# A step of its own for the decay sums' load, and 56 stores issued from ScalarE's queue

## The chip, the core and the metric

The kernel runs on one core of a Trainium2 chip. The core has a matrix engine (TensorE, PE in the profile), a vector engine (VectorE, DVE), an activation engine (ScalarE, ACT), GpSimd (POOL) and a queue engine that only issues transfers (SyncE, SP). Each engine works through its own list of instructions in order and waits on semaphores for the others. The metric is device time in microseconds (us): lower is better.

## What is computed

One layer over 128 context tokens and 1024 latent tokens. The part that the change touches, cut from the reference:

```
p = h @ w_in   -> [fourier_in | fourier_gate | ssd_z | ssd_xBC | dt | merge_gate_f | merge_gate_s]
f_out = ((fourier_mix(u_f) @ fnet_w) * silu(g_f)) @ w_branch_f
# state-space branch, per chunk c of 128 tokens, group g, head r, both directions:
acs   = cumsum(dt * a)                                # the decay sums
lmat  = exp(where(tri, acs[l] - acs[s], -inf))        # the masked decay
y     = (C_l . B_s) * lmat * xdt  +  C_l . state_in * exp(acs)
s_out = grouped_rmsnorm((y + xs * d_skip) * silu(z)) @ w_branch_s
merged = sigmoid(mg_f) * f_out + sigmoid(mg_s) * s_out
```

The final states of the context (`new_state_ssd_*`) are outputs too; the kernel stores them as `sout`, one tile for each of the 8 groups.

## The kernel before

All products are made of float32 values split in a high and a low part, three matmuls for one (`mm3`, L99). Every column block of `w_in` goes through `gemm` (L206): 24 steps of three matmuls, 128x384, for each third of the 1152 tokens. Between steps it calls `tick()` (L202), which advances a clock and runs whatever was booked for that time with `at(step, ticks)` (L192): the step is a generator, and each tick that it was given runs it to its next `yield`. This fixes the order of TensorE's instructions. The other engines, SP among them, get their order from a scheduler at build time, which works from what the code issued, its data and its buffers.

The state-space part is a loop over 8 groups (L643). In each, `states` (L542) makes the running states and, for k = -1, the context's final state: ScalarE copies it from PSUM to `so` (L557) and a transfer stores it (L558). `outputs` (L568) makes the outputs of one chunk in three steps: (1) load the decay sums `ab` (512 KB, broadcast over the partitions) and the factors `ea`, mask `ab` into `e` on GpSimd (L582, L583), eight exponentials on ScalarE (L586), and add the two directions on VectorE (L587); (2) multiply by `cb`; (3) the matmuls `po` and `y` (L597, L605). The nine chunks of a group come in the order 0, 4, 5, 3, 6, 2, 7, 1, 8, three ticks apart. The tiles `ab` and `so` share two buffers, and `e` has three (shared with `xhl`), `ea` three.

`gate_out` (L160) takes a gate's products from PSUM: ScalarE writes tanh into `gt`; for kind "f" (the Fourier gates, 24 tiles) VectorE then finishes it, for kind "m" (the merge gates, 48 tiles) ScalarE's result is final. Each tile of 192 KB is stored to DRAM (L168). Five merge gates are computed before the groups, one with group 4, two with group 5, one each with groups 6 and 7, and six after the last group, beside the first work of the Fourier stage (L685 on).

All transfers but nine loads from GpSimd's queue are issued from SP's queue. They are given eight completion counters in turn (DMAHW0 to DMAHW7); a transfer that takes a counter waits until the transfer that had it last has landed, unless that is known already.

Of the kernel before, what the change touches and what calls it, by code (L numbers as in the profile page):

```python
# [24 lines left out]
TH = 384  # L25
# [37 lines left out]
def tile_step(ctx, tc, a, o):  # L63
    nc = tc.nc

    ctx.enter_context(tc.manual_schedule(engines={mybir.EngineType.PE}))
    V, S, G, PE = nc.vector, nc.scalar, nc.gpsimd, nc.tensor
# [4 lines left out]
    def act(out, in_, func, bias=0.0, scale=1.0, **kw):  # L72
        S.activation(out, in_, func, bias=bias, scale=scale, **kw)  # L73

    def stt(out, in0, scalar, in1, op0, op1):
        V.scalar_tensor_tensor(out, in0, scalar, in1, op0=op0, op1=op1)

    def tt(out, in0, in1, op):
        V.tensor_tensor(out, in0, in1, op=op)
# [38 lines left out]
    def gt_(name, n=TH + 1):  # L118
        return gq.tile([P, TH + 2], F32, tag="gt", name=name)[:, 0:n]
# [40 lines left out]
    def gate_out(g, it):  # L160

        chunk, kind, dst, i = g
        for t, ps in it:
            gt = gt_(f"gt{chunk}_{t}", TH)
            act(gt, ps, AF.Tanh, scale=0.5)
            if kind == "f":
                stt(gt, gt, 1.0, ps, ALU.add, ALU.mult)
            nc.sync.dma_start(dst[i][:, t * TH : (t + 1) * TH], gt)  # L168

    def gate(n):  # L170
        for _ in range(min(n, len(gates))):
# [20 lines left out]
    def at(step, *ticks):  # L192

        for t in ticks:
            events[clock[0] + t].append(step)
# [40 lines left out]
    with pool("sp") as sp:  # L236
# [84 lines left out]
        for j in range(8):  # L321
            a8, b32 = j // 2 % 2 * 8, j % 2 * 32
            for n0, r0, nr, c0, nc_ in ((0, 1, 3, 0, 32), (96, 0, 1, 1, 15), (111, 4, 1, 1, 15)):
                dst = perm[:, j, n0 : n0 + nr * nc_].rearrange("p (r c) -> p r c", c=nc_)
# [6 lines left out]
                if cols[0] == 0:  # L331
                    G.tensor_copy(dst[:, :, 0:1], rg[:, rs_, 0:1])
                    dst, cols = dst[:, :, 1:], cols[1:]
# [141 lines left out]
    with pool("sd") as sd, pool("ss") as ss, pool("sx", side="right") as sx:  # L475
# [66 lines left out]
        def states(g, k, xb, bn, sts):  # L542

            cf, cb = (0, 0) if k < 0 else (1 + k, 8 - k)
            xw = ss.tile([P, 2, 256], F32, tag="xw", name=f"xw{g}_{k}", bufs=1)
            xhl = ss.tile([P, 2, 2, 256], F32R, tag="e", name=f"xhl{g}_{k}", bufs=3)
            xh, xl = xhl[:, 0], xhl[:, 1]
            for d, c in ((0, cf), (1, cb)):
                tt(xw[:, d].rearrange("p (j h q) -> p j h q", j=2, h=2), xb[:, c].rearrange("p (j h q) -> p j h q", j=2, h=2),
                   wsv[:, c, d, g, :].rearrange("p (h j) -> p j h", h=2).unsqueeze(3).broadcast_to([P, 2, 2, 64]), ALU.mult)  # L550
            split(xh, xl, xw)
            yield
            ps = gps(f"st{g}_{k}")
            if k < 0:
                mm3(ps, (bn[:, 0, 0], bn[:, 1, 0]), [x.rearrange("p d q -> p (d q)") for x in (xh, xl)], True, True)
                so = ss.tile([P, 1024], F32, tag="ab", name=f"so{g}", bufs=2)[:, 0:512]
                S.copy(so, ps)  # L557
                nc.sync.dma_start(o["sout"][g], so)  # L558
                return
            st = sts[0]  # L560
            for d, c in ((0, cf), (1, cb)):
                mm3(ps[:, d * 256 : d * 256 + 256], (bn[:, 0, c], bn[:, 1, c]), (xh[:, d], xl[:, d]), True, True)
            tt(st[:, k + 1].rearrange("p d (h q) -> p d h q", h=4), st[:, k].rearrange("p d (h q) -> p d h q", h=4),
               decv[:, :, g, :, k].unsqueeze(3).broadcast_to([P, 2, 4, 64]), ALU.mult)
            sv = st[:, k + 1].rearrange("p d q -> p (d q)")
            tt(sv, sv, ps, ALU.add)

        def outputs(g, c, bt, ct, xs, xb, st):  # L568

            cc = slice(col(c), col(c) + P)  # L570
            ab = ss.tile([P, 2, 4, P], F32, tag="ab", name=f"ab{g}_{c}", bufs=2)
            nc.sync.dma_start(ab.rearrange("p d h l -> p d (h l)"),
                              d_acs[c].rearrange("(d g q) l -> g d (q l)", d=2, g=NG)[g].partition_broadcast(P))
            if c > 0:

                ea = ss.tile([P, 2, 2, P], F32, tag="ea", name=f"ea{g}_{c}", bufs=3)
                for r0 in range(2):
                    nc.sync.dma_start(ea[r0 * 64 : r0 * 64 + 64].rearrange("p d j l -> p d (j l)"),
                                      d_eac[c].rearrange("(d g h j) l -> g h d (j l)", d=2, g=NG, h=2)[g, r0].partition_broadcast(64))
            e = ss.tile([P, 2, 4, P], F32, tag="e", name=f"e{g}_{c}", bufs=3)  # L580

            G.affine_select(e[:, 0], ab[:, 0], [[0, 4], [1, P]], ALU.is_ge, -1e30, base=0, channel_multiplier=-1)  # L582
            G.affine_select(e[:, 1], ab[:, 1], [[0, 4], [-1, P]], ALU.is_ge, -1e30, base=0, channel_multiplier=1)  # L583
            for d in range(2):
                for h in range(4):
                    act(e[:, d, h], e[:, d, h], AF.Exp, bias=knv[:, c, d, g, h : h + 1])  # L586
            tt(e[:, 0], e[:, 0], e[:, 1], ALU.add)  # L587
            yield
            pcb = gps(f"cb{g}_{c}")
            PE.matmul(pcb[:, 0:P], bt[:, cc], ct[:, cc], start=True, stop=True)  # L590
            tt(e[:, 0], e[:, 0], pcb[:, 0:P].unsqueeze(1).broadcast_to([P, 4, P]), ALU.mult)
            yield
            if c > 0:
                po = gps(f"po{g}_{c}")
                for d, k in ((0, c - 1), (1, 8 - c)):
                    for j in range(2):
                        PE.matmul(po[:, (2 * d + j) * P : (2 * d + j + 1) * P], st[:, k, d, j * P : j * P + P],  # L597
                                  ct[:, cc], start=True, stop=True)
                tt(ea, po.rearrange("p (d j l) -> p d j l", d=2, j=2), ea, ALU.mult)
                G.tensor_tensor(ea[:, 0], ea[:, 0], ea[:, 1], op=ALU.add)  # L600
            py = gps(f"y{g}_{c}")
            for j in range(2):
                for h in (2 * j, 2 * j + 1):
                    r0 = (h % 2) * 64
                    PE.matmul(py[r0 : r0 + 64, j * P : j * P + P], xb[:, c, h * 64 : h * 64 + 64], e[:, 0, h % 2 * 2 + j],  # L605
                              start=True, stop=True, tile_position=(0, r0))
            tt(xs[:, :, cc], xs[:, :, cc], py[:, 0 : 2 * P].rearrange("p (j l) -> p j l", j=2), ALU.add)
            if c > 0:
                tt(xs[:, :, cc], xs[:, :, cc], ea[:, 0], ALU.add)
# [33 lines left out]
        for g in range(NG):  # L643
            bt = ss.tile([P, PADW + 1], F32, tag="bt", name=f"bt{g}")
            ct = ss.tile([P, PADW + 1], F32, tag="ct", name=f"ct{g}")
            xs = sx.tile([P, 2, PADW + 1], F32, tag="xs", name=f"xs{g}")
            xb = ss.tile([P, NCH, 256], F32, tag="xb", name=f"xb{g}")
            bn = ss.tile([P, 2, NCH, P], F32R, tag="bn", name=f"bn{g}")
            sts = []
            conv_silu(B0 + g, g, bt, f"b{g}")  # L650
            for i, c0 in enumerate((0, 4, 8)):
                at(tr_b(g, c0, bt, bn), 16 + i)
            for j in range(2):
                conv_silu(XS0 + 2 * g + j, 16 + 2 * g + j, xs[:, j], f"x{g}{j}")
            for i, c0 in enumerate((0, 2, 4, 6, 8)):
                at(tr_x(g, c0, xs, xb), 11 + i)
            at(skip(g, xs), 16)
            for k in range(-1, 7):
                at(states(g, k, xb, bn, sts), 17 + 3 * k, 21 + 3 * k)
            conv_silu(C0 + g, 8 + g, ct, f"c{g}")  # L660
            st = ss.tile([P, 8, 2, 256], F32, tag="st", name=f"st{g}")
            sts.append(st)
            nc.sync.dma_start(st[:, 0], a["s0"][g])

            for i, c in enumerate((0, 4, 5, 3, 6, 2, 7, 1, 8)):
                t = 20 + 3 * i
                at(outputs(g, c, bt, ct, xs, xb, st), t - 6, t - 3, t)
            done = clock[0] + t
            gate(GATES[g])

            for j in range(2):
                for t, ps in gemm(a["w_in"][Z0 + 2 * g + j], hT, f"z{g}{j}"):
                    zt = gt_(f"zt{g}{j}{t}", TH)
                    act(zt, ps, AF.Tanh, scale=0.5)
                    stt(zt, zt, 1.0, ps, ALU.add, ALU.mult)
                    at(gated(t, xs[:, j], zt), max(0, done - clock[0]) + 1)
            pss = []
            t0 = max(0, done - clock[0]) + 2
            for t in range(3):
                at(norm(g, t, xs, pss), t0 + 3 * t, t0 + 4 + 3 * t)  # L680
# [4 lines left out]
    with ExitStack() as c2:  # L685
# [14 lines left out]
        xs = folded("xs")[0:16]  # L700
# [448 lines left out]
```

## Time and profile before

| | us |
|---|---|
| median of 3 runs | 1731.98 (1730.68 to 1734.61) |
| profiled execution | 1733.38 |
| its span | 1731.6 |
| PE busy | 1706.1 (99%) |
| VectorE busy | 1093.1 (63%) |
| ScalarE busy | 809.8 (47%) |
| GpSimd busy | 184.7 (11%) |

The span is the time between the first and the last instruction in the profile; the profiled execution has 1.8 us around it. TensorE's granted clock is at its upper level in all 40 slices of the page. A busy engine with 99% leaves 25.5 us in which TensorE did nothing; which wait ended those is what there is to look up.

### The profile page before, as it was taken

What the parts mean: (1) busy time and instruction counts of PE and PEld (TensorE: products, weight loads), DVE (VectorE), ACT (ScalarE), POOL (GpSimd) and SP (SyncE); (2) the same over time, 40 slices, a digit from 0 to 9 for tenths busy, and PEclk for the clock granted to TensorE, in tenths of its full rate; (3) what the DMA queues carried; (4) which work ended last, traced back from release to release, by engine and by line L of the source; (5) the groups of instructions that cost most, each with busy time, mean ns of one, the idle gap of its engine ahead of it and who ended that gap; (6) DMA issues with size and microseconds to landing.
All of it is one profiled execution on the core that took longest, in us unless ns stands there. A gap on an engine that the chain in (4) does not pass through costs nothing.

```text
span 1731.6 us, 27916 instructions
## 1 busy us (share of the span) xinstructions
PE 1706.1 (99%) x10728; PEld 1641.4 (95%) x10728; DVE 1093.1 (63%) x1876; ACT 809.8 (47%) x1666; POOL 184.7 (11%) x266
## 2 busy tenths in 40 slices
PE   7999999999999999999999999999999999999998
PEld 5999999999999999999999999999988999999987
DVE  6665877866857757757757758687487324444432
ACT  5445665565566576566466565415333211112221
POOL 1200210300300300301301202402000000000000
PEclk9999999999999999999999999999999999999999
DMA  9242633523524624524523525461066646643432
GB/s 349 80 102 59 152 103 104 142 92 99 149 76 114 140 70 118 141 77 114 135 75 106 140 77 146 148 228 54 16 214 217 229 146 229 220 168 120 161 122 73
DMA packets 110136, 229.63 MB, mean 133 GB/s; under 512 B 20594, under 2 KB 56436, under 8 KB 108340
## 3 DMA queue, kind: packets, MB, share of 16 engines
q1 hardware_dynamic: 108708, 223.14, 42.7%
q0 software_dynamic: 1296, 4.72, 0.7%
q8 instruction: 84, 1.38, 0.3%
q14 instruction: 48, 0.39, 0.1%
HBM read 187.24 MB, written 40.58 MB: 132 GB/s over the span
## 4 chain that ended last, share of the span: by engine, by line
PE 93%; DMA 3%; DVE 2%; issue 1%; ACT 0%; POOL 0%; SPq 0%; DVEq 0%; POOLq 0%; ACTq 0%
PE mm_g L101 5%; PE mm_g L103 5%; PE mm_g L102 5%; PE mm_x L101 4%; PE mm_x L103 4%; PE mm_x L102 4%; PE mm_z L101 3%; PE mm_z L103 3%; PE mm_z L102 3%; PE po L597 2%; PE y L605 2%; PE mm_b L101 2%; PE mm_c L101 2%; PE mm_b L103 2%; PE mm_c L103 2%; PE mm_b L102 2%
## 5 line engine op out<-in xcount | busy, mean ns | idle before, releaser
L73 ACT ACTIVATE e<-e,kwN 128x128 f32<-128x128 f32 x576 | 179.3, 390 | 110.9 <-POOL e L582 108.6
L101 PE MATMUL mm_g<-hT,wh_g 128*128 128x384 f32 x528 | 182.1, 345 | 0.0
L103 PE MATMUL mm_g<-hT,wl_g 128*128 128x384 f32 x528 | 177.9, 337 | 0.0
L102 PE MATMUL mm_g<-hT,wh_g 128*128 128x384 f32 x528 | 177.5, 336 | 0.0
L582 POOL TENSOR_SCALAR_AFFINE_SELECT e<-ab 128x512 f32<-128x512 f32 x72 | 51.0, 709 | 790.0 <-PE st L103 659.2
L101 PE MATMUL mm_z<-hT,wh_z 128*128 128x384 f32 x384 | 133.9, 349 | 0.0
L101 PE MATMUL mm_x<-hT,wh_x 128*128 128x384 f32 x384 | 131.5, 342 | 0.0
L103 PE MATMUL mm_z<-hT,wl_z 128*128 128x384 f32 x384 | 129.4, 337 | 0.0
L103 PE MATMUL mm_x<-hT,wl_x 128*128 128x384 f32 x384 | 129.2, 337 | 0.0
L102 PE MATMUL mm_x<-hT,wh_x 128*128 128x384 f32 x384 | 129.0, 336 | 0.0
L102 PE MATMUL mm_z<-hT,wh_z 128*128 128x384 f32 x384 | 129.0, 336 | 0.0
L101 PEld LDWEIGHTS mm_g<-hT,wh_g 128*128 128x128 f32 x528 | 99.3, 188 | 0.5 <-issue 0.2
L102 PEld LDWEIGHTS mm_g<-hT,wh_g 128*128 128x128 f32 x528 | 99.4, 188 | 0.4
L103 PEld LDWEIGHTS mm_g<-hT,wl_g 128*128 128x128 f32 x528 | 99.1, 188 | 0.0
L101 PEld LDWEIGHTS mm_z<-hT,wh_z 128*128 128x128 f32 x384 | 72.3, 188 | 0.9 <-issue 0.9
L101 PEld LDWEIGHTS mm_x<-hT,wh_x 128*128 128x128 f32 x384 | 72.1, 188 | 0.3
L102 PEld LDWEIGHTS mm_z<-hT,wh_z 128*128 128x128 f32 x384 | 72.3, 188 | 0.0
L102 PEld LDWEIGHTS mm_x<-hT,wh_x 128*128 128x128 f32 x384 | 72.3, 188 | 0.0
L103 PEld LDWEIGHTS mm_z<-hT,wl_z 128*128 128x128 f32 x384 | 72.1, 188 | 0.0
L103 PEld LDWEIGHTS mm_x<-hT,wl_x 128*128 128x128 f32 x384 | 72.1, 188 | 0.0
L597 PE MATMUL po<-ct,st 128*128 128x128 f32 x512 | 67.4, 274 | 0.0
L597 PEld LDWEIGHTS po<-ct,st 128*128 128x128 f32 x512 | 66.2, 191 | 0.0
(420 smaller groups left out, 4734.7 us busy)
## 6 DMA issues: line engine op xcount, KB each, us to landing
ab<-d_acs SPq DMA_DIRECT2D x72, 512.0 KB, 5.6
ea<-d_eac SPq DMA_DIRECT2D x128, 128.0 KB, 3.6
wr_g<-in_w_in SPq DMA_DIRECT2D x24, 512.0 KB, 5.5
yr<-d_y SPq DMA_DIRECT2D x16, 576.0 KB
aw<-in_ada_ss SPq DMA_DIRECT2D x8, 1024.0 KB, 5.2
wr_x<-in_w_in SPq DMA_DIRECT2D x16, 512.0 KB, 4.2
wr_z<-in_w_in SPq DMA_DIRECT2D x16, 512.0 KB, 3.6
d_y<-xs SPq DMA_DIRECT2D x16, 512.0 KB, 2.6
```

What stands on the lines that cost most here:

```text
L73: S.activation(out, in_, func, bias=bias, scale=scale, **kw)
L101: PE.matmul(ps, lhs[0], rhs[0], start=first, stop=False)
L102: PE.matmul(ps, lhs[0], rhs[1], start=False, stop=False)
L103: PE.matmul(ps, lhs[1], rhs[0], start=False, stop=last)
L582: G.affine_select(e[:, 0], ab[:, 0], [[0, 4], [1, P]], ALU.is_ge, -1e30, base=0, channel_multiplier=-1)
L597: PE.matmul(po[:, (2 * d + j) * P : (2 * d + j + 1) * P], st[:, k, d, j * P : j * P + P], ct[:, cc], start=True, stop=True)
L605: PE.matmul(py[r0 : r0 + 64, j * P : j * P + P], xb[:, c, h * 64 : h * 64 + 64], e[:, 0, h % 2 * 2 + j], start=True, stop=True, tile_posit ...
```

## The change

Two things. The load of `ab` gets a `yield` of its own, so `outputs` has four steps, and is booked at t - 9, t - 6, t - 3 and t instead of t - 6, t - 3 and t: the load is issued by the code three ticks (one chunk) ahead of its masks. And the transfers that store what ScalarE itself wrote (48 `gt` tiles of kind "m" and 8 `so` tiles) are issued from ScalarE's queue. The 24 stores of kind "f" stay with SP.

```diff
@@ gate_out
-            nc.sync.dma_start(dst[i][:, t * TH : (t + 1) * TH], gt)
+
+            (nc.sync if kind == "f" else S).dma_start(dst[i][:, t * TH : (t + 1) * TH], gt)
@@ states
                 S.copy(so, ps)
-                nc.sync.dma_start(o["sout"][g], so)
+                S.dma_start(o["sout"][g], so)
@@ outputs
             nc.sync.dma_start(ab.rearrange("p d h l -> p d (h l)"),
                               d_acs[c].rearrange("(d g q) l -> g d (q l)", d=2, g=NG)[g].partition_broadcast(P))
+            yield
             if c > 0:
@@ the loop over the groups
-                at(outputs(g, c, bt, ct, xs, xb, st), t - 6, t - 3, t)
+                at(outputs(g, c, bt, ct, xs, xb, st), t - 9, t - 6, t - 3, t)
```

TensorE's order is the same, row by row, in both programs. What moves on the other engines stands in the following places. Lines after the change are one or two higher than before.

SP, in group 5, from the load for chunk 0 on (`ab5_7` is group 5, chunk 7), before:

```order
L572 DMA ab5_3_8358<-d_acs_77 128x2x512
L168 DMA d_mf_83<-gt72_1_8268 128x384
L572 DMA ab5_6_8433<-d_acs_77 128x2x512
L168 DMA d_mf_83<-gt72_2_8385 128x384
L578 DMA ea5_6_8435<-d_eac_78 64x2x256 x2
L572 DMA ab5_2_8502<-d_acs_77 128x2x512
L179 DMA wr_x60_8968<-in_w_in 128x1024
L572 DMA ab5_7_8561<-d_acs_77 128x2x512
L578 DMA ea5_2_8504<-d_eac_78 64x2x256 x2
L572 DMA ab5_1_8618<-d_acs_77 128x2x512
L578 DMA ea5_7_8563<-d_eac_78 64x2x256 x2
L572 DMA ab5_8_8684<-d_acs_77 128x2x512
```

The same place after the change:

```order
L573 DMA ab5_3_8307<-d_acs_77 128x2x512
L573 DMA ab5_6_8379<-d_acs_77 128x2x512
L580 DMA ea5_6_8435<-d_eac_78 64x2x256 x2
L573 DMA ab5_2_8454<-d_acs_77 128x2x512
L180 DMA wr_x60_8968<-in_w_in 128x1024
L573 DMA ab5_7_8523<-d_acs_77 128x2x512
L580 DMA ea5_2_8504<-d_eac_78 64x2x256 x2
L573 DMA ab5_1_8582<-d_acs_77 128x2x512
L573 DMA ab5_8_8639<-d_acs_77 128x2x512
L580 DMA ea5_7_8563<-d_eac_78 64x2x256 x2
```

The two stores are gone and the load of `ab5_8` stands ahead of that of `ea5_7`; the rest stands as it did. Groups 4 and 5 alone have such a swap; in the other groups only stores leave the list.

GpSimd, in group 5, from the masks of chunk 2 on, before:

```order
L582 AFFINE_SELECT e5_2_8507<-ab5_2_8502 128x512
L583 AFFINE_SELECT e5_2_8507<-ab5_2_8502 128x512
L600 TENSOR_TENSOR ea5_3_8360<-ea5_3_8360 128x256
L582 AFFINE_SELECT e5_7_8566<-ab5_7_8561 128x512
L583 AFFINE_SELECT e5_7_8566<-ab5_7_8561 128x512
```

The same place after the change:

```order
L584 AFFINE_SELECT e5_2_8507<-ab5_2_8454 128x512
L585 AFFINE_SELECT e5_2_8507<-ab5_2_8454 128x512
L584 AFFINE_SELECT e5_7_8566<-ab5_7_8523 128x512
L602 TENSOR_TENSOR ea5_3_8360<-ea5_3_8360 128x256
L585 AFFINE_SELECT e5_7_8566<-ab5_7_8523 128x512
```

The sum over `ea5_3` moved behind the first mask of chunk 7, and so the second mask stands behind it.

ScalarE, at the end of the first two gates (`w_dt` is the weight of the step that TensorE does next), before:

```order
L73 ACTIVATE gt_0_672<-mm_g_0_225 128x384
L73 ACTIVATE gt_1_675<-mm_g_1_226 128x384
L73 ACTIVATE gt_2_678<-mm_g_2_227 128x384
L73 ACTIVATE gt_0_681<-mm_g_0_228 128x384
L73 ACTIVATE gt_1_684<-mm_g_1_229 128x384
L73 ACTIVATE gt_2_687<-mm_g_2_230 128x384
L89 CAST w_dt<-wr_dt 128x8x64
```

The same place after the change:

```order
L73 ACTIVATE gt_0_672<-mm_g_0_225 128x384
L73 ACTIVATE gt_1_675<-mm_g_1_226 128x384
L169 DMA d_mf<-gt_0_672 128x384
L169 DMA d_mf<-gt_1_675 128x384
L73 ACTIVATE gt_2_678<-mm_g_2_227 128x384
L73 ACTIVATE gt_0_681<-mm_g_0_228 128x384
L169 DMA d_mf<-gt_2_678 128x384
L169 DMA d_mf<-gt_0_681 128x384
L73 ACTIVATE gt_1_684<-mm_g_1_229 128x384
L73 ACTIVATE gt_2_687<-mm_g_2_230 128x384
L169 DMA d_mf<-gt_1_684 128x384
L169 DMA d_mf<-gt_2_687 128x384
```

Six stores now stand ahead of the cast of `w_dt`.

ScalarE, in the third gate from the last, with the semaphores that each row waits for, after the change (before, the same rows stand without the stores):

```order
L73 ACTIVATE gt78_0_11621<-mm_g78_0_11596 128x384 [waits DVE_49,PE_49]
L169 DMA d_ms_84<-gt78_0_11621 128x384 [waits DMAHW4_49,Activation_49]
L73 ACTIVATE gt78_1_11649<-mm_g78_1_11624 128x384 [waits DVE_49,PE_49]
L169 DMA d_ms_84<-gt78_1_11649 128x384 [waits DMAHW6_49,Activation_49]
L89 CAST wh_g80_11771<-wr_g80_11772 128x1024 [waits DMAHW3_49,DVE_49,PE_49]
```

Each store waits for ScalarE's own result and for a counter; in the built program the one that DMAHW4 counts here is SP's load of `xe` (L722 before), and DMAHW6 SP's load of two rows of `odd0` (L745 before).

## Rows read from the trace of the kernel before

**Rows 1.** The page, part 1: busy us, share of the span, instructions.

```profile
PE 1706.1 (99%) x10728; PEld 1641.4 (95%) x10728; DVE 1093.1 (63%) x1876; ACT 809.8 (47%) x1666; POOL 184.7 (11%) x266
```

**Rows 2.** Waits of PE, whole span: waiter, releaser, us in total, times, longest.

```profile
PE ps_s L266 <- DVE sq L79: 9.0, 1, 9.0
PE y L605 <- DVE e L79: 4.4, 5, 1.7
```

**Rows 3.** Stretches of groups 4, 5: length, busy PE PEld DVE ACT POOL, clock, DMA, GB/s.

```profile
683.00:733.00 50.00, 50.00 (x357) 47.24 (x356) 39.68 (x71) 25.60 (x75) 17.15 (x24) 1.00 0.61 154
810.00:862.00 52.00, 50.28 (x358) 47.48 (x357) 39.07 (x69) 25.61 (x76) 17.62 (x24) 1.00 0.55 144
```

**Rows 4.** Waits of SP's queue, whole span.

```profile
SPq L168 <- ACT gt L73: 110.2, 30, 20.2
SPq L572 <- POOL e L583: 87.2, 40, 6.1
SPq L572 <- DMA out_sout<-so: 15.0, 8, 3.1
```

**Rows 5.** Timeline of SP's queue in group 5: start us, us, what.

```profile
817.29 0.37 SPq L572 DMA_DIRECT2D ab<-d_acs  x1
822.06 0.32 SPq L168 DMA_DIRECT2D d_mf<-gt  x1
822.61 1.23 SPq L578 DMA_DIRECT2D ea<-d_eac  x2
823.94 0.54 SPq L572 DMA_DIRECT2D ab<-d_acs  x1
...
826.68 0.37 SPq L572 DMA_DIRECT2D ab<-d_acs  x1
...
832.34 1.59 SPq L578 DMA_DIRECT2D ea<-d_eac  x2
837.17 0.37 SPq L572 DMA_DIRECT2D ab<-d_acs  x1
```

**Rows 6.** Timeline of GpSimd in group 5; in brackets: idle before, and its releaser.

```profile
816.64 0.63 POOL L583 TENSOR_SCALAR_AFFINE_SELECT e<-ab 128x512 f32<-128x512 f32 x1
...
831.12 0.73 POOL L600 TENSOR_TENSOR ea<-ea 128x256 f32<-128x256 f32 x1
835.92 0.64 POOL L582 TENSOR_SCALAR_AFFINE_SELECT e<-ab 128x512 f32<-128x512 f32 x1 [4.06 <-DMA ab<-d_acs]
```

**Rows 7.** Timeline of VectorE in group 5.

```profile
839.14 0.69 DVE L79 TENSOR_TENSOR e<-e 128x512 f32<-128x512 f32 x1 [5.36 <-ACT e L73]
...
847.60 0.68 DVE L79 TENSOR_TENSOR ea<-po,ea 128x512 f32<-128x512 f32 x1
```

**Rows 8.** Timeline of ScalarE in group 5: the exponentials of chunk 7.

```profile
836.59 2.45 ACT L73 ACTIVATE e<-e,kwN 128x128 f32<-128x128 f32 x8 [3.54 <-POOL e L582]
```

**Rows 9.** Line L168: issues' ns minimum, median, maximum; first, last start; landing.

```profile
L168 SPq DMA_DIRECT2D d_mf<-gt x24: 319/320/2458, 59.0 to 822.1; - x24
L168 SPq DMA_DIRECT2D d_ms<-gt x24: 319/324/1442, 921.5 to 1168.0; - x24
...
DMA to landing us min/median/max: 1.9/2.7/4.4
```

**Rows 10.** Timelines of ScalarE and VectorE after the first two gates.

```profile
58.52 3.09 ACT L73 ACTIVATE gt<-mm_g 128x384 f32<-128x384 f32 x6 [0.94 <-PE mm_g L227]
61.51 0.61 ACT L89 CAST w_dt<-wr_dt 128x512 fp32r<-128x512 f32 x1
...
63.33 0.69 DVE L79 TENSOR_TENSOR w_dt<-wr_dt,w_dt 128x512 fp32r<-128x512 f32 x1
```

**Rows 11.** Timelines of SP's queue and ScalarE in the third gate from the last.

```profile
1137.22 0.26 SPq L722 DMA_DIRECT2D xe<-d_ev  x1
...
1133.95 0.49 ACT L73 ACTIVATE gt<-mm_g 128x384 f32<-128x384 f32 x1 [2.97 <-issue]
...
1146.51 0.49 ACT L73 ACTIVATE gt<-mm_g 128x384 f32<-128x384 f32 x1 [2.97 <-issue]
```

## The prediction

> **What bounds the kernel now.** I read the page's busy line first: TensorE works 1706.1 of the span's 1731.6 us [rows 1], and front of it stands the clock at its upper level throughout, so nothing in this change can make its work shorter. Only the 25.5 us in which it did nothing can move. So the second view is the list of what TensorE waited for [rows 2]. The largest entry, 9.0 us for `ps_s`, lies in the normalisation ahead of everything the diff touches. The only entry that the loads of `ab` reach is `y` waiting for `e`: 4.4 us in five waits, the longest 1.7. That is the ceiling of what the first half of the change can give: 4.4 of 1733, a quarter of a per cent.
>
> The third view tempts to another reading: SP's queue waited 110.2 us for `gt` tiles of ScalarE and 15.0 for landings of `so` [rows 4]. But that is idleness of a queue, and it only costs what stands behind it in the queue and is late at TensorE. To price it I went to the two places where those stores share the queue with the loads of `ab`: groups 4 and 5. In the 50 us of group 4 TensorE was busy 50.00; in 52 us of group 5, 50.28 [rows 3]. The difference there is the 1.7 us wait.
>
> **The moved load.** The diff says three ticks earlier; the order lists say that SP's rows stand as they did but for two swaps. The trace says why an earlier booking gives little: `ab` has two buffers, so a load must wait until GpSimd has masked the tile two chunks back. In group 5 the second mask of that kind ran from 816.64 for 0.63, to 817.27 [rows 6], and the load went out at 817.29 [rows 5]. 40 such waits, 87.2 us in all [rows 4], say the same of most loads. Three ticks more don't shorten this, since the buffer sets the issue and not the code. Gain: **0**. Bounds: 4.4 gained, if every wait of `y` went; the other side is the swap below.
>
> **Group 5, where SP's list changes most.** The 1.7 us go back from VectorE's sum of `e` at 839.14, which had waited 5.36 for ScalarE [rows 7], over the exponentials of chunk 7 at 836.59 [rows 8], to the first mask at 835.92, which had waited 4.06 for its load [rows 6]. That load was issued at 826.68 [rows 5] and so took 835.92 - 826.68 = 9.2 us at most, behind the transfers issued before it. Three edits touch this chain.
>
> First, the two stores leave SP's list. The one in view took 0.32 at 822.06, and the load of `ea` behind it began at 822.61 [rows 5]. Taking it away gives 0.32 to the issues behind it, if they wait for nothing else; but the load of chunk 7 at 826.68 was issued 2.2 us after the end of the row ahead of it that stands here (823.94 + 0.54) [rows 5], so it has its own reason to wait. The store's 192 KB still move, from another queue: at the 144 GB/s of this stretch [rows 3] that is some 1.4 us of transfer, which may fall ahead of the late load or behind it. Bounds -1.4 and +1.4; I take 0, because the bytes and the time of the ScalarE rows that release them are the same.
>
> Second, GpSimd's sum over `ea5_3`, 0.73 us at 831.12 in an idle stretch, now stands between the two masks of chunk 7 [rows 6]. The first mask feeds the first four exponentials, the second the other four. Eight took 2.45 from 836.59, so the first four ended near 837.81 [rows 8]. The second mask used to end at 835.92 + 2 x 0.64 = 837.20; with 0.73 more it ends at 837.93, 0.12 after ScalarE could use it. Price **+0.1** (0 to 0.73), as long as the wait in group 5 is there.
>
> Third, the load of `ea5_7` goes out behind that of `ab5_8`, so after 837.17 + 0.37 and its own 1.59 rather than at 832.34 [rows 5]: it is issued by 839.1. Its product stands at 847.60 on VectorE [rows 7], 8.5 us later, and the late load above, with its 9.2 us, is the worst example that I have for a landing; stores land in 1.9 to 4.4 [rows 9]. At the median it is covered, at the worst it is 0.7 late in a chain that VectorE, not TensorE, ends. Price 0 (0 to 0.7). Group 4 has the same swap and no wait to lengthen [rows 3]: 0.
>
> **The stores at the start.** Six stores now stand on ScalarE ahead of the cast of `w_dt`. On SP an issue took 0.32 at the median, 0.319 at the least [rows 9]: 6 x 0.32 = 1.92 us. On ScalarE no trace here shows one. The six `gt` rows took 3.09, or 0.52 each [rows 10]. The cast ended at 61.51 + 0.61 = 62.12, and VectorE came to it only at 63.33 [rows 10]: 1.2 us of cover. 1.92 - 1.21 = 0.7 would be late for TensorE's next step. Half of the issues can fall into the time in which ScalarE waits for the next product (0.94 ahead of the first row [rows 10]), so I take **+0.3** (0 to 0.7). Without the cover it would be 1.9. The far bound is in a rival.
>
> **The 50 others.** 50 x 0.32 = 16 us more on an engine that is busy 809.8 of 1731.6 [rows 1]. It delays by 0.3 at a time what stands behind: an exponential, a cast, a copy out of PSUM. The one wait that I followed back over ScalarE is that of group 5, and no store stands among the exponentials of chunk 7 there. I take 0 for 49 and **+0.1** for the last merge gate's store, with the cast of the next weights behind it. The 8 stores of `so` free SP of nothing: the load behind them still needs their landing, since `so` has the buffer that the load wants.
>
> **Counters.** A new wait is one that the diff doesn't show. A store on ScalarE waits for its completion counter, and the whole engine behind it. The worst that I found is in the third gate from the last: the first store stands behind the `gt` that began at 1133.95, and its counter was last taken by SP's load of `xe`, issued at 1137.22 [rows 11]. With the 1.9 to 4.4 us that transfers of line L168 take to land [rows 9], ScalarE stands from 1133.95 + 0.49 = 1134.4 until 1139.1 to 1141.6. Behind it are the next third's `gt` and the cast of the next weights. TensorE is hurt only once it wants the PSUM buffer again that this `gt` empties; there are three, so that is when the next gate's second third begins, about when its first third's `gt` runs, 1146.51 [rows 11]. Cover: 1146.5 - 1141.6 = 4.9 us. Price **0**, and a rival if the cover fails.
>
> **Sum.** 0 + 0.1 + 0.3 + 0.1 + 0 = +0.5 us. The profiled execution took 1733.38, so 1733.9 after it. It is 1.4 above the median of the runs, 1731.98; carried to the median the forecast is **1732.5 us**, which is no change that can be told: 0.2%, or 3.5 us, is about what a measurement of this kernel tells from nothing (1728.5 to 1735.4).
>
> **Rivals.** *A, faster.* Without the stores SP's queue is never held up by ScalarE, and loads go out as soon as buffers are free; all five waits of `y` go: 1731.98 - 4.4 = 1727.6 us. For it: 110.2 us of waiting at L168 [rows 4]. Against it: in group 5 the store stood 0.32 in the queue, and the load that was late had been waiting for GpSimd's buffer, then for the transfers ahead of it [rows 5]; in group 4, with a gate as well, nothing was late [rows 3]. The Trainium skill's page "Perfetto Trace Analysis", section on DMA optimizations, advises one issuing engine for loads and another for stores, to spread them better; by that rule this time would come out. The Trainium skill's page "DMA: Bandwidth & Descriptors", section "Issuing engines are not separate DMA queues", speaks against the gain: only issue time is saved, and the transfers share the same engines.
>
> *B, slower: ScalarE held at a counter.* The mechanism is the one above, at the load of `xe`. It decides from the point at which `xe` lands after 1146.5 less the two rows that must follow (0.49 each [rows 11]), so 8.3 us after its issue where stores take 4.4 at most [rows 9]; the load of chunk 7 took up to 9.2. SP's row may also come later than 1137.22, as it follows other rows in its queue. 4 us past that point gives 1736, and the same again in a second gate 1740. For it: the counter in the built program. Against: 3.9 us of room beyond the slowest landing of L168.
>
> *C, slower: issues cost more on ScalarE.* If each of the six at the start takes what the longest free-standing row of L168 took, 1.442 [rows 9] (2.458 contains waiting), then 6 x 1.44 - 1.21 = 7.4 us come at TensorE: 1739.4. For it: nothing shows an issue on ScalarE. Against: medians of 0.320 and 0.324 for the same transfer.
>
> *D: the change doesn't do what it says.* The loads don't go out earlier in the program; this is the forecast itself, and gives its time.
>
> **How the numbers follow.** Forecast 0.78; A 0.07; B 0.09; C 0.06. The forecast's own bounds, against before, are -1.4 and 1.4 + 0.7 + 0.7 + 0.7 + 0.1 = +3.6: 1730.6 to 1735.6; the runs of before went from 1730.68 to 1734.61, so the median can move by a us or so by itself. With half of A and the near end of B the range is 1729 to 1736. Faster by over 0.2%: most of A, 0.06. Slower: B and C, 0.15. Within: 0.79.
>
> **What would show it.** The waits of `y` for `e` should stay near 4.4 in five or six waits; if they are gone, A is right and my reading of the buffers wrong. Loads of `ab` should still go out within 0.1 us of the masks that free their buffer, and SP's wait for `gt` should fall to the waits of the "f" gates' neighbours without TensorE's idle time falling with it. On ScalarE the rows of L169 should be near 0.32; 1 us or more would be C. ScalarE should stand idle some 5 us behind the `gt` at 1134 with a transfer as its releaser, and TensorE's wait list should have no new entry there; an entry of `mm_g` waiting for `gt` is B. The cast of `w_dt` should end near 64, and TensorE's next step begin 0 to 0.7 later. In group 5 the second mask of chunk 7 should follow the sum over `ea`, and TensorE's wait stay near 1.8. A stretch of group 4 with TensorE under full would refute the zero for the swaps.

## The result, and the profile after it

The changed kernel took **1743.03 us** at the median of four runs (1741.54 to 1744.55), the kernel before 1731.81 beside it (1730.68 to 1734.61): a ratio of 1.0052, with an interval of 1.0036 to 1.0069. (The ratios here and below are not quotients of the medians beside them, and can differ from those by a tenth of a per cent.) It is slower by half a per cent, clear of the runs' spread, and above the predicted range of 1729 to 1736. The profiled execution has a span of 1742.8 us. On the page and in TensorE's waits this stands where [rows 1, 2] stood (busy us, share, instructions; waiter, releaser, us in total, times, longest):

```profile
PE 1711.5 (98%) x10728; PEld 1645.8 (94%) x10728; DVE 1098.3 (63%) x1876; ACT 810.7 (47%) x1666; POOL 183.2 (11%) x266
```

```profile
PE ps_s L267 <- DVE sq L79: 8.8, 1, 8.8
PE y L607 <- DVE e L79: 8.0, 5, 3.3
PE ps_a L291 <- DMA aw<-in_ada_ss: 2.1, 2, 1.4
PE ns L631 <- ACT qh L89: 1.6, 1, 1.6
```

TensorE does the same 10728 matmuls, yet was busy 5.4 us longer; its waits for `e` went from 4.4 to 8.0 us; and a wait is there that before had no row, `ns` for `qh`. (`q` are the squares that the state-space branch's normalisation sums up, `qh` and `ql` their high and low part, and `ns` the matmul that sums them, in three thirds of the tokens.) Since its order is the same in both, the n-th matmul of one trace can be set beside the n-th of the other. The difference of their starts grows in steps:

| place | later by (us) | what |
|---|---|---|
| groups 0 to 2 | 0.22 | |
| group 3, chunk 2 | 2.60 | 1.03 waiting, 1.57 at the lower clock behind it |
| group 4, chunk 2 | 0.45 | a wait that was not there |
| group 5, chunk 2 | 4.14 | 1.60 waiting, 2.54 at the lower clock |
| group 7 | 0.94 | waiting |
| `ns` behind group 7 | 2.19 | 1.77 waiting for `qh` and `ql`, the rest in the two rows of `ns` |
| behind it | 0.62 | |

The sum is 11.16, the two spans' difference 11.2. Two things in it I had not looked for. **The lower clock.** Stretches of the kernel after (length, busy PE PEld DVE ACT POOL, granted clock, DMA share, GB/s), in groups 3 and 5:

```profile
588.00:592.00 4.00, 3.55 (x19) 3.41 (x20) 3.18 (x7) 2.32 (x8) 1.42 (x3) 0.70 0.73 196
846.00:851.00 5.00, 4.16 (x18) 3.86 (x19) 4.33 (x8) 2.62 (x8) 2.46 (x4) 0.50 0.58 131
```

and TensorE's timeline there (start, us, what; in brackets the idle time before and its releaser):

```profile
846.84 1.12 PE L607 MATMUL y<-e,xb 128*64 128x128 f32 x8 [3.32 <-DVE e L79]
...
849.13 0.52 PE L103 MATMUL mm_z<-hT,wl_z 128*128 128x384 f32 x1
849.45 0.52 PE L101 MATMUL mm_z<-hT,wh_z 128*128 128x384 f32 x1
849.77 0.52 PE L102 MATMUL mm_z<-hT,wh_z 128*128 128x384 f32 x1
```

Behind the 3.32 us in which TensorE waited, matmuls start every 0.32 us; 0.50 of full speed is the level of 1.2 GHz. In the kernel before, the 1.72 us wait at this place was followed by four microseconds at full clock:

```profile
842.00:846.00 4.00, 4.00 (x28) 3.83 (x29) 3.80 (x8) 2.75 (x10) 2.50 (x3) 1.00 0.35 69
```

So a wait could cost more than its length, here 1.60 more of waiting and 2.54 behind it. The two stretches at the lower clock, 1.57 and 2.54, are 4.1 of the 5.4 us by which TensorE was busy longer. The length of the wait alone does not tell whether the clock falls: the experiments' traces have it fallen behind waits of 1.76 (e2, group 0) and 1.41 us (e11, at `ns`), and still up behind 1.77 (the changed kernel, group 7) and 2.27 us (e6, group 7).

**The sums of `wu`.** Behind group 7, GpSimd forms a sum and a difference of the Fourier stage's first weights. Before, it did so from 1112.34, with VectorE's `wl_g` and `q` done by then. The timelines of SP's queue, GpSimd and VectorE in the kernel before:

```profile
1104.84 0.35 SPq L168 DMA_DIRECT2D d_ms<-gt  x1
1105.70 0.35 SPq L179 DMA_DIRECT2D wr_g<-in_w_in  x1
1106.14 0.38 SPq L801 DMA_DIRECT2D wu<-in_wuT  x1
```

```profile
1112.34 2.40 POOL L802 TENSOR_TENSOR wu<-wu 128x1024 f32<-128x1024 f32 x1 [12.20 <-DMA wu<-in_wuT]
...
1104.45 1.23 DVE L79 TENSOR_TENSOR wl_g<-wr_g,wh_g 128x1024 fp32r<-128x1024 f32 x1 [1.50 <-ACT wh_g L89]
1105.67 0.56 DVE L79 TENSOR_TENSOR q<-q,q 128x386 f32<-128x386 f32 x1
```

and after the change, where TensorE is 8.35 us later at this place:

```profile
1106.91 0.35 SPq L803 DMA_DIRECT2D wu<-in_wuT  x1
...
1112.29 2.40 POOL L804 TENSOR_TENSOR wu<-wu 128x1024 f32<-128x1024 f32 x1 [3.82 <-DMA wu<-in_wuT]
1114.77 3.25 POOL L805 TENSOR_TENSOR wu<-wu 128x1024 f32<-128x1024 f32 x1
...
1112.79 2.98 DVE L79 TENSOR_TENSOR wl_g<-wr_g,wh_g 128x1024 fp32r<-128x1024 f32 x1 [1.50 <-ACT wh_g L89]
1115.70 2.74 DVE L79 TENSOR_TENSOR q<-q,q 128x386 f32<-128x386 f32 x1
```

The load of `wu` stood behind a store that waited for its `gt` until 1104.84. Without the store it left at 1106.91 - 8.35 = 1098.56 of the old time, 7.6 us earlier, and GpSimd's sums ran beside VectorE's two rows. These took 2.98 and 2.74 us instead of 1.23 and 0.56; `qh`, cast from `q`, was late, and TensorE waited 1.61 and 0.16 us for `qh` and `ql`. The Trainium skill's page "SBUF — State Buffer", section "Who interferes with whom", says that a VectorE operation with both inputs in SBUF contends with a GpSimd operation that reads SBUF. The trace agrees, with 1.75 and 2.18 us more for VectorE's rows and 0.85 for GpSimd's second.

### The profile page after: what moved, and what is told of

The parts are those of the page before. It is cut to its first block, busy times and chain, and to the rows that moved or that the text cites. A ratio compares the mean times of both kernels' runs of the same rounds, so it can differ in the third digit from the quotient of the medians.

```text
span 1742.8 us, 27877 instructions
## 1 busy us (share of the span) xinstructions
PE 1711.5 (98%) x10728; PEld 1645.8 (94%) x10728; DVE 1098.3 (63%) x1876; ACT 810.7 (47%) x1666; POOL 183.2 (11%) x266
## 3 DMA queue, kind: packets, MB, share of 16 engines
q8 instruction: 84, 1.38, 0.3%
## 4 chain that ended last, share of the span: by engine, by line
PE 91%; DMA 4%; DVE 2%; issue 1%; ACT 1%; POOL 0%; SPq 0%; ACTq 0%; DVEq 0%; POOLq 0%
PE mm_g L101 5%; PE mm_g L103 5%; PE mm_g L102 5%; PE mm_x L101 4%; PE mm_x L103 4%; PE mm_x L102 4%; PE mm_z L101 3%; PE mm_z L103 3%; PE mm_z L102 3%; DMA ab<-d_acs 2%; PE po L599 2%; PE y L607 2%; PE mm_b L101 2%; PE mm_c L101 2%; PE mm_b L103 2%; PE mm_c L103 2%
```

## The experiments

The theory at this point, **W**: what belongs to the change is the meeting at `wu`, 2 us, and a later landing of chunk 7's load in groups 4 and 5; the rest are late landings that can come in any of these kernels, with the lower clock behind them. The rivals: the moved load itself, the stores everywhere, or all of the 11 us as a fixed cost of the change (rival A below; the letters are those of the expectations, not of the prediction). e1 to e4, e5 to e8 and e9 to e12 ran on three different chips, each time with the kernel before beside them:

| kernel | median us (12 runs) | before, same chip (35 runs) | ratio and interval |
|---|---|---|---|
| e1 step only | 1735.62 | 1734.91 | 1.0017 (0.9995 to 1.0039) |
| e2 `d_ms` from SP | 1734.46 | 1734.91 | 1.0010 (0.9994 to 1.0026) |
| e3 `d_mf` from SP | 1737.43 | 1734.91 | 1.0019 (1.0003 to 1.0035) |
| e4 `sout` from SP | 1738.99 | 1734.91 | 1.0026 (1.0007 to 1.0045) |
| e5 the change again | 1737.06 | 1733.89 | 1.0023 (1.0008 to 1.0037) |
| e6 `wu` from ScalarE | 1741.30 | 1733.89 | 1.0029 (1.0012 to 1.0047) |
| e7 three `ab` | 1728.75 | 1733.89 | 0.9963 (0.9948 to 0.9979) |
| e8 three `ab`, the change | 1731.11 | 1733.89 | 0.9980 (0.9963 to 0.9997) |
| e9 three `ab` again | 1727.93 | 1734.56 | 0.9959 (0.9942 to 0.9976) |
| e10 `d_mf`, `sout` moved | 1728.29 | 1734.56 | 0.9961 (0.9945 to 0.9977) |
| e11 `d_ms` moved | 1729.83 | 1734.56 | 0.9968 (0.9953 to 0.9984) |
| e12 no sums of `wu` | 1730.33 | 1734.56 | 0.9970 (0.9954 to 0.9987) |

**The step alone.**

```diff
+            yield
             if c > 0:
...
-                at(outputs(g, c, bt, ct, xs, xb, st), t - 6, t - 3, t)
+                at(outputs(g, c, bt, ct, xs, xb, st), t - 9, t - 6, t - 3, t)
```

> The load's own step and its earlier booking alone; all stores on SP's queue as before. Theory S (the stores' queue is the cause): all five engines' lists read as those of the kernel before, so the time is that of before, 1731.8 within 2 us, and the waits of y for e stay near 4.4 us in five. Rival L (the moved load is the cause, since earlier loads collide with others): the time goes to about 1743 and the waits to about 8.0 us.

All five engines' lists are those of the kernel before, row for row, and TensorE's waits for `y` are of the same kind:

```profile
PE y L607 <- DVE e L79: 3.1, 4, 1.3
```

Rival L falls: the step by itself moves no row. That the buffers set the place of the loads is the prediction's reading of it, which the third buffer below bears out. The runs taught something else. This program, the same as before, took 1731.13 to 1750.79 us, and the 35 runs of the kernel before 1729.31 to 1745.87. On this chip a difference of 10 us between two runs says little.

**Parts of the stores back on SP.** In e2 those of `d_ms`, in e3 those of `d_mf` (the same line with `d_mf`), in e4 those of `sout`:

```diff
-            (nc.sync if kind == "f" else S).dma_start(dst[i][:, t * TH : (t + 1) * TH], gt)
+            (nc.sync if kind == "f" or dst is d_ms else S).dma_start(dst[i][:, t * TH : (t + 1) * TH], gt)
```

> The change, but the 24 stores of the last eight merge gates (d_ms) issued from SP again; those of d_mf and the sout stores stay on ScalarE. Theory W: without those stores SP's load of wu goes out some 8 us earlier against TensorE, and GpSimd's sums of wu (2.40 and 3.25 us from 1112.29) meet VectorE's wl_g and q, which took 2.98 and 2.74 us instead of 1.23 and 0.56. So here VectorE's two rows are back at 1.2 and 0.6, TensorE's wait of 1.6 us for qh is gone, and the time is about 2.2 us under that of the change: 1740 to 1741.5. Rival (VectorE was held by something else): the wait for qh stays and the time is 1743.

VectorE's two rows are back, and no wait of `ns` for `qh` is left:

```profile
1105.33 1.23 DVE L79 TENSOR_TENSOR wl_g<-wr_g,wh_g 128x1024 fp32r<-128x1024 f32 x1 [1.51 <-ACT wh_g L89]
1106.55 0.56 DVE L79 TENSOR_TENSOR q<-q,q 128x386 f32<-128x386 f32 x1
```

The mechanism came out. The time expected from the first result, 1740 to 1741.5, did not; on this chip none of the kernels' medians is more than 4.1 us over the kernel before.

> The change, but the 24 stores of the first eight merge gates (d_mf) issued from SP again; those of d_ms and sout stay on ScalarE. Theory S: group 5's chunk 7 loses its lengthened landing (10.7 us, 9.2 before) and the wait of 3.3 us goes back to 1.7, TensorE's granted clock stays at the upper level there, and the time is 4 to 5 us under that of the change: 1738 to 1739. Rival N (landings differ by a us from load to load, whatever the stores do): the wait in group 5 stays over 2.5 us, or it falls and others grow, and the time stays within 1.5 us of 1743.

The wait in group 5 fell, to 0.28 us. But group 0 had one of 5.06, where the load of chunk 7 landed late (GpSimd, then TensorE):

```profile
215.89 0.64 POOL L584 TENSOR_SCALAR_AFFINE_SELECT e<-ab 128x512 f32<-128x512 f32 x1 [7.46 <-DMA ab<-d_acs]
...
222.33 1.12 PE L607 MATMUL y<-e,xb 128*64 128x128 f32 x8 [5.06 <-DVE e L79]
...
224.62 0.52 PE L103 MATMUL mm_z<-hT,wl_z 128*128 128x384 f32 x1
```

From its issue to its mask this load took 12.2 us; in the traces of e1, e2 and e4 it took 7.8, 8.8 and 8.0. The matmuls behind the wait are again at 0.52. So single loads land late, in different groups from trace to trace. That speaks for rival N for most of the 11 us, though neither theory's time came, as in e2. And `ns` did not wait for `qh`, with the stores of `d_ms` still on ScalarE. In this trace the load of `wu` took 7.2 us from its issue to the sums, in the changed kernel's 5.4, and the sums began when `wl_g` was done and `q` had just begun (GpSimd, then VectorE):

```profile
1110.27 2.81 POOL L804 TENSOR_TENSOR wu<-wu 128x1024 f32<-128x1024 f32 x1 [5.66 <-PE ns L631]
...
1108.93 1.23 DVE L79 TENSOR_TENSOR wl_g<-wr_g,wh_g 128x1024 fp32r<-128x1024 f32 x1 [1.51 <-ACT wh_g L89]
1110.25 0.56 DVE L79 TENSOR_TENSOR q<-q,q 128x386 f32<-128x386 f32 x1
```

Two later rows of VectorE were long instead (2.89 and 2.75 us), and TensorE waited 0.41 us, for `ql`. So the 2 us are not there in every execution of a kernel with these stores; they come when the sums meet `wl_g` and `q`. What is the stores' own is smaller: with those of `d_mf` on ScalarE, chunk 7's load in group 4 took 7.4 to 8.2 us (the changed kernel, e2, e4, e5, e6), with them on SP 6.5 to 6.7 (before, e1, e3). The two rows that bound it after the change, SP's and GpSimd's:

```profile
703.03 0.36 SPq L573 DMA_DIRECT2D ab<-d_acs  x1
...
710.79 0.64 POOL L584 TENSOR_SCALAR_AFFINE_SELECT e<-ab 128x512 f32<-128x512 f32 x1 [2.78 <-DMA ab<-d_acs]
```

> The change, but the eight sout stores issued from SP again; the 48 gate stores stay on ScalarE. If ScalarE's sout stores delay the loads of ab in group 3 (wait 2.05 us against 1.01, then the lower clock), the wait there falls to about 1.0, the clock stays up, and the time is 2.6 us under the change: about 1740.4. If they don't matter (the loads behind them wait for the same landing either way), the wait in group 3 stays near 2 us and the time at 1743.

The wait in group 3 was 1.29 us instead of 2.05, and one in group 7 was 3.95 instead of 1.77, with the lower clock behind it: inconclusive on `sout`, and one more case of a late landing that moved.

**The change again, and `wu` held back.**

> The change itself again, in a fuller sample on the chip of this call. Theory W (a part that is there in every run: VectorE's rows of 2.98 and 2.74 us beside GpSimd's sums of wu, 2.1 us of TensorE's time, plus chunk 7's later landings in groups 4 and 5, 0.5 to 1 us each; the rest of the 11 us are late landings of single loads, which any of these kernels can have, with the lower clock that follows them): 3 to 5 us over the kernel before of the same call, and the wait of ns for qh near 1.5 us again. Rival A (all of the 11 us belongs to the change): 9 to 12 us over it.

1737.06 against 1733.89, 3.2 us more at the medians (4.0 by the ratio, with an interval of 1.4 to 6.4): within what W said, and rival A, 9 to 12 us, falls on this chip. The trace has the waits of `y` at 3.4 us and the meeting at `wu` whole:

```profile
PE y L607 <- DVE e L79: 3.4, 3, 1.4
PE ns L631 <- ACT qh L89: 1.7, 1, 1.7
```

```diff
-            nc.sync.dma_start(wu[:, 0:2], a["wuT"][g])
+            S.dma_start(wu[:, 0:2], a["wuT"][g])
```

> The change, with the four loads of wu issued from ScalarE's queue, where the first stands behind the cast of qh in the seventh group, some 6 us later against TensorE than from SP. Theory W: GpSimd's sums of wu then start behind VectorE's wl_g and q, these take 1.2 and 0.6 us, TensorE doesn't wait 1.5 us for qh, and the time is 2 us under that of the change in the same call. Rival: the wait for qh has another cause and stays.

It failed as a cure, and shows the same meeting once more. The sums started later against TensorE, but the second pair followed at once, and VectorE's `wl_g`, too, had come later, as ScalarE's cast of `wh_g` now stood behind a `gt` and two rows of `q`:

```profile
1107.36 2.40 POOL L804 TENSOR_TENSOR wu<-wu 128x1024 f32<-128x1024 f32 x1 [5.62 <-PE mm_g L103]
1109.84 3.20 POOL L805 TENSOR_TENSOR wu<-wu 128x1024 f32<-128x1024 f32 x1
1113.01 2.70 POOL L804 TENSOR_TENSOR wu<-wu 128x1024 f32<-128x1024 f32 x1
...
1107.55 3.29 DVE L79 TENSOR_TENSOR wl_g<-wr_g,wh_g 128x1024 fp32r<-128x1024 f32 x1 [0.38 <-ACT wh_g L89]
1110.76 2.70 DVE L79 TENSOR_TENSOR ql<-q,qh 128x386 fp32r<-128x386 f32 x1
1113.38 2.87 DVE L83 TENSOR_SCALAR xs<-xs,rcol 16x1024 f32<-16x1024 f32 x1
```

Now three rows of VectorE in a row are long, and TensorE's wait moved to `ql`: 2.64 us, with the lower clock behind it.

**A third buffer for `ab`.** It takes the room of one of the six that `gt` and `q` share, so this kernel differs from the one before in both.

```diff
-    gq = right.enter_context(pool("gq", 6, side="right"))
+    gq = right.enter_context(pool("gq", 5, side="right"))
...
-                so = ss.tile([P, 1024], F32, tag="ab", name=f"so{g}", bufs=2)[:, 0:512]
+                so = ss.tile([P, 1024], F32, tag="ab", name=f"so{g}", bufs=3)[:, 0:512]
...
-            ab = ss.tile([P, 2, 4, P], F32, tag="ab", name=f"ab{g}_{c}", bufs=2)
+            ab = ss.tile([P, 2, 4, P], F32, tag="ab", name=f"ab{g}_{c}", bufs=3)
```

> The kernel before with three buffers for ab instead of two, and five instead of six for gt to make room; stores on SP and no step added. Theory B (the buffers, not the place in the code, set when ab is loaded): each load goes out about one chunk, 4 to 7 us, earlier, the waits of y for e fall from 4.4 us to under 1, with them the stretches at the lower clock, and the time is 2 to 5 us under the kernel before. Rival D (the transfers themselves are too slow, 512 KB beside the others): an earlier issue lands hardly earlier, and the waits stay over 3 us.

The time is 0.9963 of the kernel before, with twelve runs between 1725.46 and 1730.39 where the 35 of before lie between 1728.69 and 1743.32. No wait of `y` is left in TensorE's list. Against `y` of chunk 2 in group 5, chunk 2's load leaves 22.9 us ahead instead of 18.0, chunk 7's 16.3 instead of 15.3, and so 6.6 us behind the other instead of 2.7. Its mask waits for ScalarE now, not for the load; SP, then GpSimd:

```profile
821.87 0.55 SPq L572 DMA_DIRECT2D ab<-d_acs  x1
...
828.95 0.64 POOL L582 TENSOR_SCALAR_AFFINE_SELECT e<-ab 128x512 f32<-128x512 f32 x1 [2.27 <-ACT e L73]
```

Against [rows 6], where the same mask had waited 4.06 us for the load. Theory B holds, and this kernel beats both.

> The change with the same three buffers for ab and five for gt. Theory W and B: the waits of y are gone as in the kernel before with three buffers, and what is left against that one is the wait for qh beside GpSimd's sums, about 2 us. Rival A: with the stores on ScalarE it is 8 us or more above it.

1731.11 - 1728.75 = 2.4 us over e7. Set beside the trace of before, the two traces gain the same at chunk 2 of groups 3, 5 and 7 (1.1, 1.8 and 1.0 us each), and part at `ns`, where only e8 loses, 1.56 + 0.41. Theory W holds, rival A falls.

**Which stores.** The last four have e7's three buffers; e10 has the line of e2, e11 this one, with `sout` back on SP:

```diff
-            (nc.sync if kind == "f" else S).dma_start(dst[i][:, t * TH : (t + 1) * TH], gt)
+            (S if dst is d_ms else nc.sync).dma_start(dst[i][:, t * TH : (t + 1) * TH], gt)
```

> The kernel before with three buffers for ab and five for gt again, as the base of this call: with no late landings in its way it shows a us or two. 1728.7 within 1.5 us, no waits of y for e over 0.4 us.

> Three buffers for ab, and on ScalarE's queue only the 24 stores of d_mf and the eight of sout; the 24 of d_ms stay with SP. Theory W: the time is that of the base within 0.7 us, with no wait of ns for qh. Rival (the earlier stores on ScalarE cost something in every group): it stands 1.5 us or more over the base.

> Three buffers for ab, and on ScalarE's queue only the 24 stores of d_ms. Theory W: all of the stores' cost is here: 2 to 2.6 us over the base, a wait of ns for qh of 1.3 to 1.7 us, and VectorE's wl_g and q near 2.7 us each beside GpSimd's sums. Rival: the time of the base within 0.7 us.

The base is at 1727.93, with no wait of `y`. e10 is 0.4 above it, with no wait of `ns`; e11 is 1.9 above it, just under the 2 to 2.6 expected, with the wait and the long rows of VectorE (2.72 and 2.75):

```profile
PE ns L631 <- ACT qh L89: 1.4, 1, 1.4
```

So with the landings covered, the 32 earlier stores cost nothing that can be told, and the 24 late ones cost the 2 us. In e11's trace the clock fell behind this wait of 1.41 us, to 0.50 of full speed from 1107 to 1110; in e8, behind 1.38 us at the same place, it did not.

```diff
-            G.tensor_tensor(wu[:, 2], wu[:, 0], wu[:, 1], op=ALU.add)
-            G.tensor_tensor(wu[:, 0], wu[:, 0], wu[:, 1], op=ALU.subtract)
+            nc.sync.dma_start(wu[:, 2], a["wuT"][g][:, 0])
```

> Three buffers for ab and all 56 stores on ScalarE, as in the eighth kernel, without GpSimd's sum and difference of wu (left out: the third row is loaded as a copy of the first). Theory W (it is GpSimd's sums beside VectorE, not the stores or the loads, that make VectorE's rows long): wl_g and q take 1.2 and 0.6 us, ns waits no more for qh, and the time is within 0.7 us of the base. Rival T (the transfers that leave earlier are what holds VectorE or TensorE up): the wait stays and the time is 2 us over the base.

The kernel leaves out the two sums. Half of what was expected came. VectorE's rows are short, with the stores on ScalarE and the early load of `wu` as in e8, and TensorE does not wait at this place:

```profile
1099.24 1.23 DVE L79 TENSOR_TENSOR wl_g<-wr_g,wh_g 128x1024 fp32r<-128x1024 f32 x1 [1.50 <-ACT wh_g L89]
1100.57 0.56 DVE L79 TENSOR_TENSOR q<-q,q 128x386 f32<-128x386 f32 x1
```

So it is the sums, not the stores or the loads, that made them long. But the time is 2.4 us over the base, and `ns` waits 1.4 us again, in the next third of the tokens. ScalarE shows where that comes from:

```profile
1099.63 0.33 ACTq L169 DMA_DIRECT2D d_ms<-gt  x1
...
1102.94 0.49 ACT L73 ACTIVATE gt<-mm_g 128x384 f32<-128x384 f32 x1 [1.20 <-PE mm_g L103]
1106.60 0.52 ACT L73 ACTIVATE q<-xs 128x382 f32<-128x382 f32 x1 [3.17 <-DMA d_ms<-gt]
1106.66 0.33 ACTq L169 DMA_DIRECT2D d_ms<-gt  x1
```

It is `q` that waits, 3.17 us, and what releases it is the landing of a store already on its way, the one of 1099.63: `q` and `gt` take their buffers from the same pool (`gt_`, L118), so `q` cannot be written until the store that reads its buffer has landed. In e8 that store left at 1098.66, and the same `q` began at 1104.53 without a wait. What differs is the traffic. Without its sums GpSimd issues its eight loads of `xf` 22 us earlier than in e8; e12, then e8:

```profile
1094.86 0.70 POOL L706 DMA_DIRECT2D xf<-in_xf  x1
1095.99 3.64 POOL L706 DMA_DIRECT2D xf<-in_xf  x7 [0.43 <-DVE xs L79]
...
1116.61 4.36 POOL L706 DMA_DIRECT2D xf<-in_xf  x8
```

Between 1094 and 1114 the core's queues moved 382 GB/s in e12 and 161 in e8. So the new wait is most likely the experiment's own: transfers that it brought forward, beside the store. No run separates that. Rival T falls at the place that it was about, where the stores and the early load of `wu` are there and the wait is not; its words (the wait stays, 2 us over the base) came true by another wait, a third of the tokens later. But e12's time does not price the meeting at `wu`: the 2 us rest on e8 against e7 and e11 against e9.

## Why the prediction was wrong

**What bounds the kernel: the reading failed in one sentence.** SP's 110.2 us of waiting at L168 [rows 4] were called "idleness of a queue", to be priced in groups 4 and 5 alone. I did not ask what the held queue kept back elsewhere. Behind group 7 a store that waited kept back the load of `wu`, and with it GpSimd's sums, until VectorE was through with `wl_g` and `q`. That delay was worth about 2 us (2.4 in e8 against e7, 1.9 in e11 against e9, and 2.19 in the changed kernel's trace); the term is not in the sum at all. The instruction that I should have followed is the next one in SP's list at each removed store.

**The ceiling of 4.4 us was no ceiling.** It counted the waits of one trace, and not the lower clock that can follow one, nor that another execution of the same kernel can have longer waits. With three buffers no wait of `y` is left, and the gain is 5.1 us (1733.89 - 1728.75) and 6.6 us (1734.56 - 1727.93) at the medians. The same holds for losses: 1.60 us more of waiting in group 5 cost 4.14, and the four steps at `y` in the table are 8.1 of the 11.2 us. The prediction's bounds for group 5, 1.4 + 0.7 + 0.7, left no room for that. The prediction let only the 25.5 us of TensorE's idleness move; its busy time moved too, by 5.4.

**The moved load: right.** Price 0, and e1 shows that not a row moved. The prediction's rival A, faster at 1727.6 us, fell: SP no longer waits for ScalarE's `gt`, but its waiting for the masks, 87.2 us [rows 4], became

```profile
SPq L573 <- POOL e L585: 111.6, 40, 6.2
```

**The stores' own transfers: mis-sized.** I took 0 in bounds of 1.4, and 0 for group 4 since nothing waited there. Chunk 7's landing there became about 1 us later, and a wait of 0.4 to 0.8 us appeared in the traces of the change, e2, e4 and e6, though not in e5's. The sum over `ea` between the two masks of group 5 costs the 0.12 predicted, as far as the trace can tell: the load took 10.7 us instead of 9.2, 1.48 later, and TensorE was 1.60 later.

**The start: right, and the cover held.** An issue on ScalarE takes 0.326 us at the median, so rival C falls. The cast of `w_dt` began at 62.67 instead of 61.51, 1.16 later where the prediction had 1.92 less what falls into ScalarE's waiting, and VectorE took it up at 63.33, as before; price 0 rather than 0.3.

**The counter: right.** ScalarE stood from 1145.04, when `gt` was done, to 1150.36, 5.3 us where the prediction had 4.7 to 7.2, and no wait of TensorE followed. SP had issued the load of `xe`, which had this counter before, at 1145.98:

```profile
1145.98 0.26 SPq L724 DMA_DIRECT2D xe<-d_ev  x1
...
1144.55 0.49 ACT L73 ACTIVATE gt<-mm_g 128x384 f32<-128x384 f32 x1 [2.92 <-PE mm_g L103]
1150.36 0.33 ACTq L169 DMA_DIRECT2D d_ms<-gt  x1
1150.79 0.49 ACT L73 ACTIVATE gt<-mm_g 128x384 f32<-128x384 f32 x1 [5.75 <-DVE odd L76]
```

The prediction expected a transfer as the releaser of the row behind; the profile names VectorE's `odd`, the later of two waits. In e5 the store stood 8.0 us there without a wait of TensorE, so rival B did not come true at this place.

**What stays open.** By e5 the change costs 3.2 us at the medians (1.4 to 6.4 by its interval), of which some 2 are shown at `wu`; that is no more than the range allowed over the kernel before (1736 - 1731.98 = 4.0), so there the time would have lain in the range with the term at `wu` still missing, which would have been luck. In the first comparison it was 11.2, and all four of its runs lay over all four of before. Its trace puts 8.1 of that to late landings and the clock behind them, which e3 and e4 show in other groups and which a third buffer takes away. Why the first four runs were all that slow, whether the change makes such landings more frequent, and what makes a load land 1 to 4 us late, no run here settles.

## What to carry to other kernels

An instruction that waits in a queue also holds back what stands behind it; before taking it out, follow the next rows of that queue to the engines that they release, and see what these will run beside. To start a load earlier, count its buffers first: here one more buffer was worth 5 to 7 us at the medians, and an earlier place in the code nothing. When an experiment leaves work out, look at what moves up into the gap before its time is read as a price. Take several runs of both kernels before explaining a difference of half a per cent.

## What the hardware showed that was not expected

- VectorE's `tensor_tensor` of 128x1024 took 2.7 to 3.3 us beside GpSimd's of the same size instead of 1.23, and one of 128x386 took 2.74 instead of 0.56.
- After waits of 1.41, 1.76, 2.05, 3.32 and 5.06 us, TensorE's granted clock was at its lower level for some microseconds; after others of 1.38, 1.72, 1.77 and 2.27 us it was not.
- The same load of 512 KB took 10.7 us from its issue to its mask in one trace of the changed kernel and 8.5 in another (group 5, chunk 7, the first trace and e5); in group 0 it took 7.8 us in e1 and 12.2 in e3.
